# The first microseconds of a two-layer encoder kernel: matmuls of ones, two requests on ACT's queue, and squares and lambda moved

## The chip, the cores and the metric

The kernel runs on one core of a Trainium2 chip. The core has a matrix engine (PE, with its weight loads shown apart as PEld), a vector engine (DVE), a scalar engine (ACT), GpSimd (POOL) and a sequencer that mostly issues transfers (SP). Each runs its own instructions in order and waits for the others by semaphores. The metric is the device time of one execution in microseconds. The kernel before takes 1100.9 us, the median of three runs from 1099.71 to 1102.21.

## What is computed

The input is 512 tokens of 1024 features. Two layers follow each other, each a mixer and an MLP with squared ReLU, with an RMS norm ahead of each and a norm at the end. All of it is float32. Cut to what matters:

```
h = rmsnorm(x, norm_mix[0])                  # even layer
q, k, v, u = split(h @ ab_w_in)
p = softmax(q1 k1) - lam * softmax(q2 k2)    # 4 heads, block-causal
lam = exp(sum(l0*l1)) - exp(sum(l2*l3)) + lam_init
x = x + concat(subln(p @ v), pool_mixer(u)) @ ab_w_out
x = x + relu(rmsnorm(x) @ w1)**2 @ w2
h = rmsnorm(x, norm_mix[1])                  # odd layer: gated linear attention (GLA)
q, k, v, g, gk = split(h @ gla_w_in)
log_a = log_sigmoid(gk @ w_up + b) / 16      # decay per key feature
o = chunked_linear_attention(q, k, v, cumsum(log_a))
x = x + (rmsnorm(o) * silu(g)) @ gla_w_out
x = x + relu(rmsnorm(x) @ w1)**2 @ w2
return rmsnorm(x, norm_final)
```

The norm's factor for a token is the same for all features, so the kernel multiplies the raw `x` (times the gain) by the weights and puts the factor `rb` on the product when it leaves PSUM.

## The kernel before

**Tiling.** `x` is held transposed, as 8 tiles of 128 features x 512 tokens, numbered by `f`. A product of two float32 matrices is made of three matmuls of a reduced type: each operand is split into a high part and the rest, and `mm3` (L149 to L151) issues high x high, high x rest and rest x high into one PSUM bank. ACT makes the high parts (`wh` at L273 and L127, `row` at L181 and L187), DVE the rests (`wl` at L274 and L128, `row` at L182 and L188). A projection of one output tile (`proj_T`) is 8 x 3 = 24 matmuls of 512 columns; weights come from memory in blocks of 1 MB that hold two such tiles.

**The head.** The first weight block and `x` are requested by SP in pieces, alternately (L100 to L103): x0, w0, x1, w1, x2-3, w2-3, x4-5, w4-7, x6-7. The first part of `par` (gains and small constants) is requested on ACT's queue (L94), the second on SP's (L104). As the pieces land, ACT and DVE split them, and PE runs the first two output tiles of the q/k projection, feature tile by feature tile (`ps0`, 48 matmuls), then two more from the next block (`ps1`, L127/L128 and L149 to L151). Beside them ACT squares `x` (L244 and L238) and DVE adds the squares up (`nacc`, L247); `nrm.rb()` splits the sum (L203/L204), PE adds it over the partitions (L205/L206), ACT makes a reciprocal square root by Ln and Exp (L217, L218) and DVE refines it (L210 to L212). Then DVE evicts the four banks (L312), PE computes the scores (L326), and the v projection begins (L173 to L175), which needs free PSUM banks. Lambda's chain (L293 to L303) requests 128 KB on SP's queue behind two blocks of v weights.

**Order.** The code is a list in program order that a scheduler reorders by priorities and by a model of durations. `soon()` raises the priority, and `tc.issue_after(i)` keeps an instruction behind `i`. Scratch tiles of 128 x 512 come from buffer sets that are named `tmp` and `row`: the helper `tmp()` gives one from the one or the other set by turns, so each call to it decides for all later calls which set they fall into. When a buffer comes free is part of what the scheduler orders by.

**The GLA layer.** Its decays are made by Abs, Exp and Ln for four heads (L729 to L738), with table loads of ACT's functions between (L735, L740); scans (L745) add them up; `weights(h)` makes exponentials and products (L754, L765 to L773), and PE transposes one of the products (L776). At the layer's end the gate projection (24 matmuls for each of 8 tiles) is followed by its eviction (L898), Silu on ACT (L902) and the product with the normed output (L903), by a table load behind the last Silu (L905), by the split of 8 tiles for the output projection (L187/L188), and by that projection (`add_out(wo1, ...)`).

Of the kernel before, what the change touches and what calls it, by code (L numbers as in the profile page):

```python
# [9 lines left out]
F32 = mybir.dt.float32  # L10
F32R = mybir.dt.float32r
U8 = mybir.dt.uint8
AF = mybir.ActivationFunctionType
ALU = mybir.AluOpType
AX = mybir.AxisListType

P = 128
S = 512
D = 1024
KB = D // P  # L20
# [5 lines left out]
LAM_INIT = 0.2  # L26
# [4 lines left out]
C_SUB, C_PSC, C_BGK, C_GN, C_ICNT, C_ID = 40, 41, 45, 49, 57, 121  # L31
# [4 lines left out]
def trunk(ctx: ExitStack, tc: tile.TileContext, xT, par, lvl, lam4, wqk0, wu0, wv0, poolw, wo0,  # L36
          wgk, wup, wqk1, wv1, wg1, wo1, w1a, w2a, w1b, w2b, gfin, out):
    nc = tc.nc
    V, A, G, PE = nc.vector, nc.scalar, nc.gpsimd, nc.tensor
# [4 lines left out]
    def T(shape, tag, bufs, dt=F32):  # L44
        cnt[0] += 1
        return sb.tile(shape, dt, tag=tag, bufs=bufs, name=f"{tag}_{cnt[0]}")
# [6 lines left out]
    def turn(name, bufs):  # L53
        ring[name] = ring.get(name, -1) + 1
        return ring[name] % bufs

    def row(n=S, dt=F32):
        return T([P, n], "row", 54, dt)
# [17 lines left out]
    def tmp(n=S, dt=F32):  # L76
        if not mlp[0] and turn("tmp", 2):
            return row(n, dt)
        return T([P, n], "tmp", 4, dt)

    def PS(tag, shape=(P, S)):
        cnt[0] += 1
        return pp.tile(list(shape), F32, tag=tag, bufs=4, name=f"ps{tag}_{cnt[0]}")
# [9 lines left out]
    prm = T([P, N_PAR], "par", 1)  # L93
    nc.scalar.dma_start(prm[:, 0:C_ICNT], par[:, 0:C_ICNT])  # L94
    xall = T([P, KB, S], "x", 1)
    x = [xall[:, f, :] for f in range(KB)]
    turn("raw", 2)
    raw0 = raws[:, 0:4 * S].rearrange("p (a n) -> p a n", a=2)
    xT3 = xT.rearrange("(f p) s -> p f s", p=P)
    for f, nx, nw in ((0, 1, 1), (1, 1, 1), (2, 2, 2), (4, 2, 4), (6, 2, 0)):  # L100
        nc.sync.dma_start(xall[:, f:f + nx, :], xT3[:, f:f + nx, :])
        if nw:
            nc.sync.dma_start(raw0[:, :, f * P:(f + nw) * P], wqk0[0, :, :, f * P:(f + nw) * P])  # L103
    nc.sync.dma_start(prm[:, C_ICNT:], par[:, C_ICNT:])  # L104
    ident = prm[:, C_ID:C_ID + P]
    ones = T([P, P], "ones", 1)
    V.memset(ones, 1.0)
    ones_r = T([P, P], "onesr", 1, F32R)
    V.tensor_copy(ones_r, ones)
    A.preload_act_table_set("natural_log_exp_and_others")  # L110


    def load(src):
# [5 lines left out]
    ended = {}  # L119
# [24 lines left out]
    def act_tiles():  # L144
        return row(dt=F32R), row(dt=F32R)

    def mm3(ps, w, a, first, last):
        (wh, wl), (ah, al) = w, a
        PE.matmul(ps, wh, ah, start=first, stop=False)  # L149
        PE.matmul(ps, wh, al, start=False, stop=False)  # L150
        ended["mm"] = PE.matmul(ps, wl, ah, start=False, stop=last).ins  # L151

    def proj_T(w, act, tag="mm", ps=None, kbs=tuple(range(KB)), first=0, last=KB - 1):

        hi, lo = w
        ps = PS(tag) if ps is None else ps
        for kb in kbs:
            c = slice(kb * P, (kb + 1) * P)
            mm3(ps, (hi[:, c], lo[:, c]), act[kb], kb == first, kb == last)
        return ps  # L160
# [17 lines left out]
    def split_scaled(src, col, tiles=None):  # L178

        ah, al = tiles or act_tiles()  # L180
        A.activation(ah, src, AF.Copy, scale=col)  # L181
        V.scalar_tensor_tensor(out=al, in0=src, scalar=col, in1=ah.bitcast(F32), op0=ALU.mult, op1=ALU.subtract)  # L182
        return ah, al

    def split(src, tiles=None):
# [83 lines left out]
    for f in range(KB):  # L269
        if f < 2 or f % 2 == 0:  # L270
            c = slice(f * P, (f + (1 if f < 2 else 2)) * P)
            for j in range(2):
                A.activation(hl[j][0][:, c], raw0[:, j, c], AF.Copy)  # L273
                V.tensor_tensor(hl[j][1][:, c], raw0[:, j, c], hl[j][0][:, c].bitcast(F32), ALU.subtract)  # L274
        act.append(split_scaled(x[f], prm[:, C_MIX0 + f:C_MIX0 + f + 1]))
    ps0 = [PS("mm"), PS("mm")]
    for kb in range(KB):
        c = slice(kb * P, (kb + 1) * P)
        for j in range(2):
            mm3(ps0[j], (hl[j][0][:, c], hl[j][1][:, c]), act[kb], kb == 0, kb == KB - 1)  # L280
    st = Stream(wqk0, 2)
    ps1 = [proj_T(st.next(), act)]
    nrm = Norm()
    for f in range(KB):
        nrm.add(x[f])
    with tc.issue_after(ended["hi"]), tc.issue_after(ended["lo"]), tc.issue_after(ended["mm"]):
        rb = nrm.rb()
    first_sum = ended["sum"]
    ps1.append(proj_T(st.next(), act))


    l4 = tmp(256)
    nc.sync.dma_start(l4, lam4.partition_broadcast(P))  # L293
    lp = tmp(128).rearrange("p (a d) -> p a d", a=2)
    l4v = l4.rearrange("p (a b d) -> p a b d", a=2, b=2)
    V.tensor_tensor(lp, l4v[:, :, 0, :], l4v[:, :, 1, :], ALU.mult)
    consts = T([P, P], "lcol", 1)
    ls, le, neglam, sub8 = (consts[:, i:j] for i, j in ((0, 2), (8, 10), (16, 17), (24, 25)))
    V.tensor_reduce(out=ls, in_=lp, op=ALU.add, axis=AX.X)
    A.activation(le, ls, AF.Exp)  # L300
    V.tensor_tensor(neglam, le[:, 1:2], le[:, 0:1], ALU.subtract)
    V.tensor_scalar(out=neglam, in0=neglam, scalar1=-LAM_INIT, scalar2=None, op0=ALU.add)
    V.tensor_scalar(out=sub8, in0=prm[:, C_SUB:C_SUB + 1], scalar1=1.0 - LAM_INIT, scalar2=None, op0=ALU.mult)  # L303

    qk = {}

# [91 lines left out]
    def pooled(i, g):  # L398
        w = POOL_W[g]
        ps = proj_T(st.next(), act)  # L400
        u = row_u()
        G.memset(u[:, 0:16], 0.0)
        with soon():
            V.tensor_tensor(u[:, 16:], ps, rb, ALU.mult)
        s, step, us = u, 1, [row_u(), row_u()]
        while step < w:
            s2 = us[0]
            us.reverse()
            G.memset(s2[:, 0:16], 0.0)
            V.tensor_tensor(s2[:, 16:], s[:, 16:], s[:, 16 - step:16 + S - step], ALU.add)  # L410
            s, step = s2, 2 * step
        r = tmp2()
        V.scalar_tensor_tensor(out=r[:, 16:], in0=s[:, 32:], scalar=1.0 / w, in1=u[:, 32:], op0=ALU.mult,
                               op1=ALU.subtract)
        V.tensor_tensor(r[:, 0:16], s[:, 16:32], prm[:, C_ICNT + 16 * g:C_ICNT + 16 * (g + 1)], ALU.mult)
        V.tensor_tensor(r[:, 0:16], r[:, 0:16], u[:, 16:32], ALU.subtract)
        psy = PS("ax")
        PE.matmul(psy, pw[:, g, :], r, start=True, stop=True)
        cat[NH + i] = split_scaled(psy, prm[:, C_PSC + g:C_PSC + g + 1], (row16(dt=F32R), row16(dt=F32R)))
# [10 lines left out]
    def add_out(arr, src, col, late):  # L430


        st = Stream(arr)
        n, nxt = Norm(), []
        kbs = tuple(kb for kb in range(KB) if kb != late)
        ws = [st.next(), st.next()]
        pss = [proj_T(w, src, kbs=kbs, first=kbs[0], last=late) for w in ws]
        for w, ps in zip(ws, pss):
            proj_T(w, src, ps=ps, kbs=(late,), first=kbs[0], last=late)
        for f in range(KB):  # L440
            ps = pss[f] if f < 2 else proj_T(st.next(), src)
            with soon():
                V.tensor_tensor(x[f], x[f], ps, ALU.add)
                nxt.append(split_scaled(x[f], prm[:, col + f:col + f + 1]))
            n.add(x[f])
        return nxt, n
# [222 lines left out]
    act, nrm = add_out(wo0, cat, C_FFN0, NH - 1)  # L669
# [8 lines left out]
    act, nrm = ffn(w1a, w2a, act, nrm, C_MIX1)  # L678
# [12 lines left out]
    for kb in range(KB):  # L691
        for j in range(2):
            PE.matmul(psg, gk2[kb // 4][:, kb % 4, :, :].rearrange("p a b -> p (a b)"), act[kb][j],
                      start=kb == 0 and j == 0, stop=kb == KB - 1 and j == 1)
# [46 lines left out]
    for e, m in zip(es, ms):  # L741
        b = row16()
# [165 lines left out]
    act, nrm = add_out(wo1, oh, C_FFN1, KB - 1)  # L908
# [86 lines left out]
```

## Time and profile before

| | |
|---|---|
| runs | 1100.9 us median, 1099.71 to 1102.21 |
| profiled execution | 1100.49 us, of which the span (first to last instruction) is 1098.7 us |
| PE busy | 1071.5 us, 98% of the span |
| DVE, ACT busy | 825.5 us, 540.9 us |
| bytes moved | 103.53 MB, 94 GB/s over the span |
| PE idle, windows 0 to 35 us | 7.3 us, of which 4.85 ahead of its first matmul |

The span is nearly all matrix work, so time can only come out of the few places where PE stands still or runs at a lower clock, and go into new ones. Times of rows are microseconds from the span's start. A matmul of 512 columns is shown as 0.39 us long, but they follow each other every 0.227 us.

### The profile page before, as it was taken

What the parts mean: (1) busy time and instruction counts of PE and PEld (TensorE: products, weight loads), DVE (VectorE), ACT (ScalarE), POOL (GpSimd) and SP (SyncE); (2) the same over time, 40 slices, a digit from 0 to 9 for tenths busy, and PEclk for the clock granted to TensorE, in tenths of its full rate; (3) what the DMA queues carried; (4) which work ended last, traced back from release to release, by engine and by line L of the source; (5) the groups of instructions that cost most, each with busy time, mean ns of one, the idle gap of its engine ahead of it and who ended that gap; (6) DMA issues with size and microseconds to landing.
All of it is one profiled execution on the core that took longest, in us unless ns stands there. A gap on an engine that the chain in (4) does not pass through costs nothing.

```text
span 1098.7 us, 12896 instructions
## 1 busy us (share of the span) xinstructions
PE 1071.5 (98%) x4968; PEld 863.5 (79%) x4968; DVE 825.5 (75%) x1234; ACT 540.9 (49%) x894; POOL 2.3 (0%) x20
## 2 busy tenths in 40 slices
PE   7999889999999999999999999999999999999997
PEld 5676558888888888888887778788888888888885
DVE  6747747696498498498869887775696696696696
ACT  6444435455354354354655466854553453453454
POOL 0000000000000000000000000000000000000000
PEclk9999989999999999999999999999999999999999
DMA  7222223213314314302222121333205206206102
GB/s 239 82 84 108 82 77 124 88 39 136 132 39 153 116 39 154 115 17 84 108 77 77 39 86 39 146 115 115 96 1 209 98 1 224 83 1 229 39 1 78
DMA packets 17918, 103.53 MB, mean 94 GB/s; under 512 B 2016, under 2 KB 3040, under 8 KB 6208
## 3 DMA queue, kind: packets, MB, share of 16 engines
q1 hardware_dynamic: 17712, 102.67, 26.0%
q8 instruction: 39, 0.64, 0.2%
q14 instruction: 23, 0.19, 0.1%
q10 hardware_dynamic: 144, 0.03, 0.0%
HBM read 100.59 MB, written 2.10 MB: 93 GB/s over the span
## 4 chain that ended last, share of the span: by engine, by line
PE 90%; ACT 4%; DVE 4%; issue 1%; DMA 1%; SPq 0%; DVEq 0%; ACTq 0%
PE psmm L150 14%; PE psmm L149 14%; PE psmm L151 14%; PE psmm L571 6%; PE psmm L572 6%; PE psmm L573 6%; PE psax L151 3%; PE psax L149 3%; PE psax L150 3%; PE psax L573 2%; PE psax L571 2%; PE psax L572 2%; PE psmm L174 2%; PE psmm L173 2%; PE psmm L175 2%; PE psax L326 1%
## 5 line engine op out<-in xcount | busy, mean ns | idle before, releaser
L127 ACT ACTIVATE wh<-wraw 128x1024 fp32r<-128x1024 f32 x230 | 243.5, 1061 | 393.4 <-PE psmm L150 160.3
L128 DVE TENSOR_TENSOR wl<-wraw,wh 128x1024 fp32r<-128x1024 f32 x230 | 280.3, 1220 | 66.3 <-ACT wh L127 62.7
L149 PE MATMUL psmm<-row,wh 128*128 128x512 f32 x736 | 289.7, 394 | 15.0 <-ACT row L187 9.0
L150 PE MATMUL psmm<-row,wh 128*128 128x512 f32 x736 | 290.0, 394 | 0.1
L151 PE MATMUL psmm<-row,wl 128*128 128x512 f32 x736 | 288.5, 392 | 0.6 <-DVE wl L128 0.6
L149 PEld LDWEIGHTS psmm<-row,wh 128*128 128x128 f32 x736 | 138.7, 189 | 46.0 <-ACT row L187 10.1
L150 PEld LDWEIGHTS psmm<-row,wh 128*128 128x128 f32 x736 | 138.8, 189 | 31.8 <-issue 1.8
L151 PEld LDWEIGHTS psmm<-row,wl 128*128 128x128 f32 x736 | 138.9, 189 | 30.5 <-issue 1.1
L571 PE MATMUL psmm<-wh,row 128*128 128x512 f32 x320 | 124.6, 389 | 0.0
L573 PE MATMUL psmm<-wl,row 128*128 128x512 f32 x320 | 124.5, 389 | 0.0
L572 PE MATMUL psmm<-wh,row 128*128 128x512 f32 x320 | 124.5, 389 | 0.0
L546 DVE TENSOR_TENSOR wraw<-wraw 128x1024 f32<-128x1024 f32 x64 | 77.2, 1217 | 0.3
L498 DVE TENSOR_TENSOR row<-row,row 128x512 fp32r<-128x512 f32 x112 | 74.7, 682 | 0.3 <-ACT row L497 0.3
L572 PEld LDWEIGHTS psmm<-wh,row 128*128 128x128 f32 x320 | 60.1, 188 | 12.5
L573 PEld LDWEIGHTS psmm<-wl,row 128*128 128x128 f32 x320 | 60.1, 188 | 12.5
L571 PEld LDWEIGHTS psmm<-wh,row 128*128 128x128 f32 x320 | 60.1, 188 | 12.4
L497 ACT ACTIVATE row<-row 128x512 fp32r<-128x512 f32 x112 | 65.8, 618 | 5.3 <-DVE row L524 5.3
L512 DVE SCALAR_TENSOR_TENSOR tmp<-psmm,rb 128x512 f32<-128x512 f32 x48 | 32.9, 685 | 45.7 <-PE psmm L151 45.7
L517 ACT ACTIVATE row<-tmp 128x256 f32<-128x256 f32 x128 | 45.8, 405 | 10.9 <-DVE tmp L512 10.6
L151 PE MATMUL psax<-row,wl 128*128 128x512 f32 x128 | 49.8, 389 | 0.0
L149 PE MATMUL psax<-row,wh 128*128 128x512 f32 x128 | 49.8, 389 | 0.0
L150 PE MATMUL psax<-row,wh 128*128 128x512 f32 x128 | 49.8, 389 | 0.0
(235 smaller groups left out, 1312.6 us busy)
## 6 DMA issues: line engine op xcount, KB each, us to landing
wraw<-in_w1a SPq DMA_DIRECT2D x16, 1024.0 KB, 4.8
wraw<-in_w2a SPq DMA_DIRECT2D x16, 1024.0 KB, 4.8
wraw<-in_w1b SPq DMA_DIRECT2D x16, 1024.0 KB, 4.8
wraw<-in_w2b SPq DMA_DIRECT2D x16, 1024.0 KB, 4.8
wraw<-in_wo SPq DMA_DIRECT2D x8, 1024.0 KB, 4.8
wraw<-in_wqk SPq DMA_DIRECT2D x7, 1024.0 KB, 4.9
wraw<-in_wv SPq DMA_DIRECT2D x6, 1024.0 KB, 4.8
wraw<-in_wg SPq DMA_DIRECT2D x4, 1024.0 KB, 4.8
```

The source lines that it names most:

```text
L127: ended["hi"] = A.activation(hi, src, AF.Copy).ins
L128: ended["lo"] = V.tensor_tensor(lo, src, hi.bitcast(F32), ALU.subtract).ins
L149: PE.matmul(ps, wh, ah, start=first, stop=False)
L150: PE.matmul(ps, wh, al, start=False, stop=False)
L151: ended["mm"] = PE.matmul(ps, wl, ah, start=False, stop=last).ins
L497: A.activation(hi, src, AF.Copy)
L498: V.tensor_tensor(lo, src, hi.bitcast(F32), ALU.subtract)
L517: A.activation(raw[name][:, j, :], r[:, th * 256:th * 256 + 256], AF.Square)
L546: V.tensor_tensor(out[k], in0[k], in1[k], ALU.subtract)
L571: PE.matmul(ps[t], hi, wh[:, cs], start=f, stop=False, skip_group_check=True)
L572: PE.matmul(ps[t], lo, wh[:, cs], start=False, stop=False, skip_group_check=True)
L573: PE.matmul(ps[t], hi, wl[:, cs], start=False, stop=l, skip_group_check=True)
```

## The change

Four things are done in the head. The requests for x2 and x3 are made apart, and those for w0 and w1 move from SP's queue to ACT's, behind `par`. The request for lambda's vectors moves up behind x6-7, into a buffer taken directly from `tmp`'s set rather than by the helper `tmp()`. Thirty matmuls of ones (128 x 128 x 128) are issued ahead of everything on PE. The squares, and lambda's chain, which is now written ahead of `nrm.rb()`, are kept behind the last split of the first 8 tiles.

```
-    for f, nx, nw in ((0, 1, 1), (1, 1, 1), (2, 2, 2), (4, 2, 4), (6, 2, 0)):
+    for f, nx, nw in ((0, 1, 1), (1, 1, 1), (2, 1, 2), (3, 1, 0), (4, 2, 4), (6, 2, 0)):
         nc.sync.dma_start(xall[:, f:f + nx, :], xT3[:, f:f + nx, :])
         if nw:
-            nc.sync.dma_start(raw0[:, :, f * P:(f + nw) * P], wqk0[0, :, :, f * P:(f + nw) * P])
+            q = nc.scalar if f < 2 else nc.sync
+            q.dma_start(raw0[:, :, f * P:(f + nw) * P], wqk0[0, :, :, f * P:(f + nw) * P])
+    l4 = T([P, 256], "tmp", 4)
+    nc.sync.dma_start(l4, lam4.partition_broadcast(P))
     nc.sync.dma_start(prm[:, C_ICNT:], par[:, C_ICNT:])
...
+    WARM = 30
     A.preload_act_table_set("natural_log_exp_and_others")
+
+    psw = PS("ax", (P, P))
+    for i in range(WARM):
+        PE.matmul(psw, ones_r, ones_r, start=True, stop=True)
...
+        ended["ah"] = A.activation(ah, src, AF.Copy, scale=col).ins
+        ended["al"] = V.scalar_tensor_tensor(out=al, in0=src, scalar=col, in1=ah.bitcast(F32), op0=ALU.mult,
+                                             op1=ALU.subtract).ins
...
+    last_split = ended["ah"], ended["al"]
     ps1 = [proj_T(st.next(), act)]
     nrm = Norm()
-    for f in range(KB):
-        nrm.add(x[f])
+    with tc.issue_after(last_split[0]), tc.issue_after(last_split[1]):
+        for f in range(KB):
+            nrm.add(x[f])
+
+        lp = tmp(128).rearrange("p (a d) -> p a d", a=2)
...
     with tc.issue_after(ended["hi"]), tc.issue_after(ended["lo"]), tc.issue_after(ended["mm"]):
         rb = nrm.rb()
     first_sum = ended["sum"]
     ps1.append(proj_T(st.next(), act))
-
-
-    l4 = tmp(256)
-    nc.sync.dma_start(l4, lam4.partition_broadcast(P))
-    lp = tmp(128).rearrange("p (a d) -> p a d", a=2)
```

Lines of the changed kernel are 8 or 9 higher than those of before (L181 becomes L189, L187 becomes L196). The rows below are the instructions of one engine in the order in which it runs them, with the numbers of the tiles.

On ACT, at the program's start, there stood before:

```order
L94 DMA par_62<-in_par 128x57
L110 ACT_TABLE_LOAD
L181 ACTIVATE row_88<-x_64,par_62 128x512
L273 ACTIVATE wh_80<-wraw_61 128x128
L273 ACTIVATE wh_82<-wraw_61 128x128
L244 ACTIVATE nacc_216<-x_64 128x512
L181 ACTIVATE row_96<-x_64,par_62 128x512
```

and now:

```order
L94 DMA par_62<-in_par 128x57
L104 DMA wraw_61<-in_wqk 128x2x128 x2
L114 ACT_TABLE_LOAD
L282 ACTIVATE wh_114<-wraw_61 128x128
L282 ACTIVATE wh_116<-wraw_61 128x128
L189 ACTIVATE row_122<-x_64,par_62 128x512
L282 ACTIVATE wh_114<-wraw_61 128x128
```

Two requests stand ahead of the table load, the two weight casts ahead of the first split of `x`, and the first square is gone from between.

Further down in the head, ACT had the Ln (L217) of the first norm ahead of the third cast of the v weights, which is the first half of the second v block:

```order
L203 ACTIVATE row_241<-nacc_216 128x512
L127 ACTIVATE wh_503<-wraw_61 128x1024
L127 ACTIVATE wh_531<-wraw_61 128x1024
L217 ACTIVATE rb_239<-psax_240 128x512
L127 ACTIVATE wh_560<-wraw_61 128x1024
L218 ACTIVATE rb_239<-rb_239 128x512
```

and now:

```order
L212 ACTIVATE tmp_283<-nacc_250 128x512
L135 ACTIVATE wh_535<-wraw_61 128x1024
L135 ACTIVATE wh_563<-wraw_61 128x1024
L304 ACTIVATE lcol_275<-lcol_275 128x2
L135 ACTIVATE wh_592<-wraw_61 128x1024
L226 ACTIVATE rb_281<-psax_282 128x512
L227 ACTIVATE rb_281<-rb_281 128x512
```

That cast (`wh_592`) is now in front of the Ln (L226).

The one call less to `tmp()` turns the sets for every scratch tile behind it, and the order changes in the GLA layer, 1000 instructions away. On ACT, at the layer's end, there stood before:

```order
L187 ACTIVATE row_5686<-row_5286 128x512
L127 ACTIVATE wh_5822<-wraw_61 128x1024
L187 ACTIVATE row_5690<-row_5298 128x512
L902 ACTIVATE wraw_61<-wraw_61 128x512
L905 ACT_TABLE_LOAD
L187 ACTIVATE row_5694<-row_5336 128x512
L187 ACTIVATE row_5698<-row_5348 128x512
L187 ACTIVATE row_5702<-row_5386 128x512
L187 ACTIVATE row_5706<-row_5398 128x512
```

and now:

```order
L196 ACTIVATE row_5710<-row_5268 128x512
L135 ACTIVATE wh_5854<-wraw_61 128x1024
L910 ACTIVATE wraw_61<-wraw_61 128x512
L913 ACT_TABLE_LOAD
L196 ACTIVATE row_5714<-row_5280 128x512
L196 ACTIVATE row_5718<-row_5318 128x512
L196 ACTIVATE row_5722<-row_5330 128x512
L196 ACTIVATE row_5726<-row_5368 128x512
L196 ACTIVATE row_5730<-row_5380 128x512
L196 ACTIVATE row_5734<-row_5418 128x512
L196 ACTIVATE row_5738<-row_5430 128x512
```

Before, four of the eight splits for the output projection ran ahead of the last Silu; now one does, and seven stand behind the table load. PE meets them behind the last matmul of the gate projection (into `psmm_5667`):

```order
L159 MATMUL psmm_5667<-row_4068,wl_5664 128x512
L157 MATMUL psmm_5751<-row_5710,wh_5743 128x512
L157 MATMUL psmm_5773<-row_5710,wh_5747 128x512
L157 MATMUL psmm_5821<-row_5710,wh_5817 128x512
L157 MATMUL psmm_5858<-row_5710,wh_5854 128x512
L158 MATMUL psmm_5751<-row_5711,wh_5743 128x512
L159 MATMUL psmm_5751<-row_5710,wl_5744 128x512
L157 MATMUL psmm_5751<-row_5714,wh_5743 128x512
L158 MATMUL psmm_5773<-row_5711,wh_5747 128x512
L158 MATMUL psmm_5751<-row_5715,wh_5743 128x512
```

Six matmuls stand between that one and the first that reads `row_5714`; before, 19 stood between the gate projection's last and the first that reads a split from behind the table load (`row_5694`). At the layer's start, the transposes of the first head (L776, now L784) stand behind 59 instructions of PE counted from the first matmul of the values' projection (into `psmm_4549`), before behind 64; and ACT makes the decays of heads 1 and 3 with both table loads first, and those of heads 0 and 2 behind them, where before all four stood between the two loads.

More of the change, by code (lines that the diff above doesn't have):

```diff
@@ L180, in split_scaled @@
         ah, al = tiles or act_tiles()
-        A.activation(ah, src, AF.Copy, scale=col)
-        V.scalar_tensor_tensor(out=al, in0=src, scalar=col, in1=ah.bitcast(F32), op0=ALU.mult, op1=ALU.subtract)
+        ended["ah"] = A.activation(ah, src, AF.Copy, scale=col).ins
+        ended["al"] = V.scalar_tensor_tensor(out=al, in0=src, scalar=col, in1=ah.bitcast(F32), op0=ALU.mult,
+                                             op1=ALU.subtract).ins
         return ah, al
@@ L281, in trunk @@
     st = Stream(wqk0, 2)
+    last_split = ended["ah"], ended["al"]
     ps1 = [proj_T(st.next(), act)]
     nrm = Norm()
-    for f in range(KB):
-        nrm.add(x[f])
+    with tc.issue_after(last_split[0]), tc.issue_after(last_split[1]):
+        for f in range(KB):
+            nrm.add(x[f])
+        lp = tmp(128).rearrange("p (a d) -> p a d", a=2)
+        l4v = l4.rearrange("p (a b d) -> p a b d", a=2, b=2)
+        V.tensor_tensor(lp, l4v[:, :, 0, :], l4v[:, :, 1, :], ALU.mult)
+        consts = T([P, P], "lcol", 1)
+        ls, le, neglam, sub8 = (consts[:, i:j] for i, j in ((0, 2), (8, 10), (16, 17), (24, 25)))
+        V.tensor_reduce(out=ls, in_=lp, op=ALU.add, axis=AX.X)
+        A.activation(le, ls, AF.Exp)
+        V.tensor_tensor(neglam, le[:, 1:2], le[:, 0:1], ALU.subtract)
+        V.tensor_scalar(out=neglam, in0=neglam, scalar1=-LAM_INIT, scalar2=None, op0=ALU.add)
+        V.tensor_scalar(out=sub8, in0=prm[:, C_SUB:C_SUB + 1], scalar1=1.0 - LAM_INIT, scalar2=None, op0=ALU.mult)
     with tc.issue_after(ended["hi"]), tc.issue_after(ended["lo"]), tc.issue_after(ended["mm"]):
@@ L289, in trunk @@
     ps1.append(proj_T(st.next(), act))
-    l4 = tmp(256)
-    nc.sync.dma_start(l4, lam4.partition_broadcast(P))
-    lp = tmp(128).rearrange("p (a d) -> p a d", a=2)
[L295 to L303, printed above, removed]
     qk = {}
```

## The prediction

> **What bounds the kernel now.** I read the page first, then PE's timeline for its idle places, then the other engines' timelines at those places, and a table by stretches for the clock. The page says that PE is nearly always busy:
>
> ```profile
> PE 1071.5 (98%) x4968; PEld 863.5 (79%) x4968; DVE 825.5 (75%) x1234; ACT 540.9 (49%) x894; POOL 2.3 (0%) x20
> ```
>
> Of the span of 1098.7 us only some 27 are not PE's, so an edit pays only where PE stands or is slow, and costs wherever it makes PE stand anew. PE's timeline (start, length, and in brackets the idle time before and what ended it) shows the places in the head:
>
> ```profile
> 4.85 0.79 PE L149 MATMUL psmm<-row,wh 128*128 128x512 f32 x1 [4.85 <-ACT wh L273]
> ...
> 8.16 0.62 PE L150 MATMUL psmm<-row,wh 128*128 128x512 f32 x1
> 8.59 0.43 PE L151 MATMUL psmm<-row,wl 128*128 128x512 f32 x1
> 8.85 0.39 PE L149 MATMUL psmm<-row,wh 128*128 128x512 f32 x1
> 9.08 0.39 PE L150 MATMUL psmm<-row,wh 128*128 128x512 f32 x1
> ...
> 10.69 0.50 PE L149 MATMUL psmm<-row,wh 128*128 128x512 f32 x1 [0.98 <-ACT wh L273]
> ...
> 21.10 0.50 PE L151 MATMUL psmm<-row,wl 128*128 128x512 f32 x1 [0.57 <-DVE wl L128]
> ...
> 32.75 0.47 PE L173 MATMUL psmm<-wh,row 128*128 128x512 f32 x1 [0.93 <-ACT wh L127]
> 33.61 1.58 PE L326 MATMUL psax<-wraw 64*128 64x128 f32 x12
> ```
>
> The first nine matmuls follow each other every 0.43 us (8.16 to 8.59), later ones every 0.23 (8.85 to 9.08): PE starts at half its clock. The wait at 32.75 is put down to ACT; by the rows below the banks that it needs were evicted only then. ACT's timeline explains the others:
>
> ```profile
> 0.73 0.41 ACTq L94 DMA_DIRECT2D par<-in_par  x1
> 1.17 1.28 ACT L110 ACT_TABLE_LOAD   x1 [1.17 <-PEq L986]
> 3.87 0.72 ACT L181 ACTIVATE row<-x,par 128x512 fp32r<-128x512 f32 x1 [1.42 <-DMA par<-in_par]
> 4.50 0.49 ACT L273 ACTIVATE wh<-wraw 128x128 fp32r<-128x128 f32 x2
> ...
> 9.09 0.72 ACT L181 ACTIVATE row<-x,par 128x512 fp32r<-128x512 f32 x1 [1.76 <-DMA x<-in_xT]
> 9.71 0.61 ACT L238 ACTIVATE tmp<-x 128x512 f32<-128x512 f32 x1
> 10.23 0.71 ACT L273 ACTIVATE wh<-wraw 128x256 fp32r<-128x256 f32 x2
> ...
> 26.87 0.60 ACT L217 ACTIVATE rb<-psax 128x512 f32<-128x512 f32 x1 [0.80 <-PE psax L206]
> ...
> 28.31 0.62 ACT L218 ACTIVATE rb<-rb 128x512 f32<-128x512 f32 x1
> ```
>
> It waits 1.76 us for the common request of x2 and x3 (9.09), then squares x2 (9.71) before it casts the weights that PE waits for at 10.69.
>
> **The requests.** Rows of SP's timeline, and from the table of transfers the median time from issue to landing:
>
> ```profile
> 1.17 0.65 SPq L103 DMA_DIRECT2D wraw<-in_wqk  x1
> ...
> 3.09 0.60 SPq L101 DMA_DIRECT2D x<-in_xT  x1
> 3.73 0.55 SPq L103 DMA_DIRECT2D wraw<-in_wqk  x1
> ...
> wraw<-in_wqk SPq DMA_DIRECT2D x2, 128.0 KB, 3.3
> wraw<-in_wv SPq DMA_DIRECT2D x2, 1024.0 KB, 4.8
> ```
>
> A request occupies its issuer some 0.6 us. With w0 and w1 gone from SP, x2 is issued near 1.8 instead of 3.09, w2-3 near 2.4 instead of 3.73. On ACT the two requests (about 1.14 to 2.4) push the table load to end near 3.7, before w0 lands (1.15 + 3.3 = 4.5), so this delay is hidden; where w0 came earlier, it would cost up to 1.2. I let w0 land at 4.4: two casts of 0.3 each, then the split (3.87 to 4.50: 0.63), so PE's first real matmul comes near **5.5**, 0.65 later than now. The bytes ahead of w2-3 are the same but for x3, which now comes behind: w2-3 should land near 9.0, f2's matmuls begin near 9.4 to 9.6, **1.2 earlier** than 10.69. From there 36 matmuls of f2 to f7 run 8.2 us; the last ends near 17.7.
>
> [...]
>
> **The thirty matmuls.** No row shows them. The smallest with weights of their own that I found are transposes of the GLA layer:
>
> ```profile
> 580.36 0.55 PE L776 MATMUL psax<-par,tmp 128*128 128x128 f32 x3 [0.27 <-DVE tmp L773]
> ```
>
> The thirty can start when the ones are cast (near 1.3) and take at least 0.107 us each (a quarter of 0.43), 3.2 us in all. At most they take 0.37 (three transposes last 0.55 at full clock, and twice that at half) until the clock rises, by 8.6 as now, and then 0.18: they end near 10.4. The nearest row is that of a chain of matmuls with a weight load each that hides it (4.85 to 8.59), so I take 0.14 (4.2 us in all): they end near 5.5, no later than the inputs. At half clock 8 matmuls cost 8 x 0.2 = 1.6 us too much now, and these would go. Most of it is hidden, though: f0 and f1, warm, are done near 8.5 and PE then waits for w2-3 until 9.4. So warm-up is worth nothing beside the 1.2, within 0 and -0.7; at the far end of the bound the 48 matmuls of f0 to f7 (10.9 us) end near 21.3 instead of 17.7, and what the rests' coming at 19.9 doesn't hide of that, 1.4, is lost.
>
> **Squares and lambda.** Six squares of 0.52 us each (9.71 to 10.23) leave the stretch of ACT from 9 to 18. DVE's part of them comes to stand in front of the weights' rests:
>
> ```profile
> 19.22 0.69 DVE L247 SCALAR_TENSOR_TENSOR nacc<-tmp,nacc 128x512 f32<-128x512 f32 x1
> 19.83 2.35 DVE L128 TENSOR_TENSOR wl<-wraw,wh 128x1024 fp32r<-128x1024 f32 x2
> ...
> 29.59 0.68 DVE L210 SCALAR_TENSOR_TENSOR row<-psax,rb 128x512 f32<-128x512 f32 x1
> 30.20 0.28 DVE L296 TENSOR_TENSOR row<-tmp 128x128 f32<-128x128 f32 x1
> ...
> 31.91 2.48 DVE L312 TENSOR_TENSOR wraw<-psmm,rb 128x512 f32<-128x512 f32 x4
> ```
>
> Five additions of 0.69 (19.22) behind the last split, which DVE ends near 15.3, are done near 18.8 to 19.1, so the first rest is ready near 19.9 against 21.0 now. The matmul that waited for it (21.10) is followed by some 46 more at 0.227, to 31.6; with as many it is near 30.4 now. What follows waits for `rb`: the Ln is, in the changed order, queued behind the cast `wh_592`, which needs the second v block. That block is requested when the rests of `ps1` are made (near 21.3) and lands 4.8 later, 26.1; cast, Ln, Exp end near 28.3, DVE's three steps of 0.61 (29.59 to 31.91 are 2.3 us with lambda's 0.28 twice (30.20) between; these go) near 30.1: evictions begin **1.8 earlier**. In the changed order the scores stand ahead of the v projection's first matmuls: they follow two evictions of 0.62, near 31.3, and 1.5 us of scores (33.61) and three matmuls of 0.227 end near 33.5, where the same work ends near 35.1 now. **Head: -1.6 us**, between -0.8 (v block at 26.9, as late as now) and -2.4.
>
> **The GLA layer.** The flipped buffers change it. The rows at its end, of ACT, DVE and PE:
>
> ```profile
> 717.99 0.62 ACT L902 ACTIVATE wraw<-wraw 128x512 f32<-128x512 f32 x1
> 718.62 1.28 ACT L905 ACT_TABLE_LOAD   x1
> 719.91 2.19 ACT L187 ACTIVATE row<-row 128x512 fp32r<-128x512 f32 x4
> 717.16 0.68 DVE L898 TENSOR_TENSOR wraw<-psmm,rb 128x512 f32<-128x512 f32 x1
> 703.88 0.50 PE L205 MATMUL psax<-row,onesr 128*128 128x512 f32 x1 [0.76 <-ACT row L203]
> 721.33 0.50 PE L150 MATMUL psmm<-row,wh 128*128 128x512 f32 x1
> ```
>
> From the last gate eviction (717.16) to the first split behind the table load (719.91 + 0.5) are 3.3 us; PE's last gate matmul started 0.9 ahead of it (19 matmuls, then the one at 720.85, back by 0.227 each: 716.3). So the chain takes some 4.1, and PE has 19 matmuls, 4.3 us, to fill it. With six (1.4) it stands 2.5 us, and 0.3 more for the first rest from DVE, less the 0.25 that it waits now (721.33): 2.6. Four matmuls of 0.227 that the changed order has ahead of the last sums, not behind, may fill the idle 0.76 there (703.88). I take **+2.2**, between +1.8 and +2.9. At its start PE comes to the transposes of 580.36 about five matmuls (1.1 us) earlier and waited already. The chain gains some 0.5 on ACT, as table loads of 1.28 (718.62) move out of its way: **+0.6**, between 0 and +1.2. One table load more lies in ACT's own waiting time (it is busy for 49% of the span); where it has none, it costs its 1.28, which the upper ends hold.
>
> **The sum** on the profiled 1100.49 (0.4 under the median of the runs): -1.6 + 2.2 + 0.6 = +1.2, **1101.7**.
>
> **The clock.** A second unknown of about 1 us each way. By stretches (busy time of each engine, then PEclk, the granted share of full clock, here 0.62, 0.53 and 0.50; the last row is PE's timeline again):
>
> ```profile
> 134.00:138.00 4.00, 0.09 (x1) 0.09 (x1) 2.87 (x5) 0.93 (x2) 0.00 (x0) 0.62 0.00 0
> 138.00:142.00 4.00, 4.00 (x6) 1.88 (x7) 2.82 (x6) 0.36 (x1) 0.00 (x0) 0.53 0.00 0
> 152.00:155.40 3.40, 3.39 (x6) 1.47 (x7) 1.40 (x4) 0.00 (x0) 0.00 (x0) 0.50 0.00 0
> 137.91 0.79 PE L149 MATMUL psmm<-row,wh 128*128 128x512 f32 x1 [4.91 <-ACT row L187]
> ```
>
> After two long waits of the attention stage PE runs some 3.8 and 3.4 us at half clock, 3.6 us lost; if all comes 1.6 earlier, these places may cost a microsecond more or less. [...]
>
> **Rivals.** (a) *The GLA places cost nothing*: the changed order fills them, only the head counts: 1100.49 - 1.6 = 1098.9, with a lucky clock 1097.9. For it: the waits there now are 0.27 (580.36), 0.76 (703.88) and 0.25; against: the split that PE needs cannot come ahead of the last Silu. Chance 0.22. (b) *The second v block is late* and the Ln behind `wh_592` with it: from a landing at 27.9 on the head gains nothing, and each further microsecond is added whole; with the GLA's 2.8 that gives 1103.3, slower. For it: the block's request waits for rests that come to stand behind five additions; against: 4.8 us is steady. Chance 0.2. (c) *The warm-up misses*: real matmuls start cold at 5.5 and stay so up to 3.4 us, 7 x 0.2 = 1.4 us, of which the wait for w2-3 hides 0.9; or the thirty end only at 10.4 (+1.4): 1102.2 to 1103.1. [...] Chance 0.13. The forecast keeps 0.45.
>
> **The numbers.** A measurement of this kernel tells 0.2% (2.2 us) from no change. The forecast's own range, -2.4 + 1.8 - 1 to -0.8 + 4.1 + 1, is 1098.9 to 1104.8, most of it within 0.2%. Half of (a) and a little of the forecast is faster: 0.2; most of (b), a third of (c) and a quarter of the forecast slower: 0.3; the rest, 0.5, the same. The range, with part of (a): 1098.3 to 1104.5.
>
> **What would show it.** PE's first real matmul at 5.3 to 5.8 and at full pitch; f2 at 9.3 to 9.7; the first L312 (then L320) near 30.1 with the Ln behind `wh_592`; scores' end near 33.5; a wait of over 2 us behind the gate projection, ended by ACT's split. I would be wrong if no such wait shows, or if the attention stage's two waits change by over a microsecond.

## The result, and the profile after

The changed kernel takes 1108.3 us (median of 6 runs, 1106.52 to 1109.96), the kernel before 1101.71 us (6 runs, 1099.71 to 1102.55): 1.0063 of it, with a 95% interval of 1.0052 to 1.0073, or 6.6 us more. The forecast was 1101.7 us in a range up to 1104.5.

| | before | after |
|---|---|---|
| profiled execution | 1100.49 us | 1109.34 us |
| its span | 1098.7 us | 1107.5 us |
| PE busy | 1071.5 us | 1080.2 us |
| DVE busy, ACT busy | 825.5, 540.9 us | 825.8, 542.6 us |

PE is busy for 8.7 us longer. Of these, 6.7 are the thirty small matmuls (the first row below), which stand where PE only waited before. The other 2.0 are the same matrix work taking longer, so part of the loss isn't waiting but matmuls at a lower clock. PE's timeline of the changed kernel, in the head:

```profile
1.31 6.67 PE L118 MATMUL psax<-onesr 128*128 128x128 f32 x30 [1.31 <-DVE onesr L112]
7.77 0.73 PE L157 MATMUL psmm<-row,wh 128*128 128x512 f32 x1
...
9.41 0.63 PE L157 MATMUL psmm<-row,wh 128*128 128x512 f32 x1
9.84 0.63 PE L158 MATMUL psmm<-row,wh 128*128 128x512 f32 x1
...
11.12 0.42 PE L158 MATMUL psmm<-row,wh 128*128 128x512 f32 x1
11.38 0.40 PE L159 MATMUL psmm<-row,wl 128*128 128x512 f32 x1
11.61 0.40 PE L157 MATMUL psmm<-row,wh 128*128 128x512 f32 x1
...
33.07 1.58 PE L334 MATMUL psax<-wraw 64*128 64x128 f32 x12 [1.09 <-DVE wraw L320]
```

Each one of the thirty takes 0.215 us (1.31 to 7.77), and they do not raise the clock: the real ones behind them still follow each other every 0.43 us (9.41 to 9.84) up to 11.1. No wait is left between 7.77 and the scores at 33.07. These begin 0.5 us earlier than before (33.61), but only because the three matmuls of the v projection that stood ahead of them now follow: the fourth starts at 35.39, where it started at 35.12 before. So the head as a whole ends 0.3 us later in this execution, not earlier. Further on, the waits of the GLA layer, in PE's timeline again:

```profile
581.86 0.55 PE L784 MATMUL psax<-par,row 128*128 128x128 f32 x3 [1.07 <-DVE row L781]
...
696.51 0.50 PE L214 MATMUL psax<-tmp,onesr 128*128 128x512 f32 x1 [1.03 <-ACT tmp L212]
...
704.65 0.71 PE L873 MATMUL psax<-row,wraw 128*128 128x128 f32 x4 [1.49 <-DVE wraw L861]
...
709.11 0.44 PE L214 MATMUL psax<-tmp,onesr 128*128 128x512 f32 x1
...
722.03 0.47 PE L157 MATMUL psmm<-row,wh 128*128 128x512 f32 x1 [0.36 <-DVE wraw L906]
724.38 0.66 PE L158 MATMUL psmm<-row,wh 128*128 128x512 f32 x1 [1.88 <-DVE row L197]
```

These waits are 5.83 us together. Before, PE waits 0.27 us at the transposes, 0.71 and 0.76 us at the two column sums of the layer's end, and 0.08 us behind the gate projection. The second of these sums (L205, now L214 at 709.11) has no wait left; the 1.49 us at 704.65 is a new wait, ahead of matmuls of the outputs. The first of the sums before:

```profile
692.72 0.50 PE L205 MATMUL psax<-row,onesr 128*128 128x512 f32 x1 [0.71 <-ACT row L203]
```

Behind the last wait of the changed kernel, the table by stretches (length, then busy time and number of instructions of PE, PEld, DVE, ACT, POOL, then the granted clock, DMA share, GB/s):

```profile
722.00:724.50 2.50, 0.59 (x2) 0.31 (x3) 2.33 (x3) 2.47 (x4) 0.00 (x0) 1.00 0.15 29
724.50:728.00 3.50, 3.50 (x9) 2.72 (x10) 3.47 (x6) 3.12 (x6) 0.00 (x0) 0.51 0.93 372
728.00:732.00 4.00, 4.00 (x19) 3.28 (x18) 0.83 (x2) 0.00 (x0) 0.00 (x0) 1.00 0.43 180
```

PE is busy for 0.59 of 2.5 us, and then runs some 3.4 us at half clock: the row counts 9 matmuls, where 3.5 us at 0.227 each hold 15. This half-clock stretch is not in the profile of before, here over the same places:

```profile
724.00:730.00 6.00, 6.00 (x28) 4.99 (x27) 2.67 (x4) 2.90 (x4) 0.00 (x0) 1.00 0.26 111
```

The start of the same matmul in both profiles, counted back from PE's last, shows where the time goes without asking what a wait is. The changed kernel's execution is 0.4 us behind after the head, 2.0 after the attention stage, 4.3 at the last matmul of the gate projection (720.60 against 716.30), and 8.3 behind the half-clock stretch and from there to the end. So the GLA layer takes 6.3 us of it: 2.3 up to the end of the gate projection and 4.0 behind it.

### The profile page after: what moved, and what is told of

Read it like the earlier page. It is cut to its first block, busy times and chain, and to the rows that moved or that the text cites. A ratio compares the mean times of both kernels' runs of the same rounds, so it can differ in the third digit from the quotient of the medians.

```text
span 1107.5 us, 12961 instructions
## 1 busy us (share of the span) xinstructions
PE 1080.2 (98%) x4998; PEld 871.0 (79%) x4998; DVE 825.8 (75%) x1234; ACT 542.6 (49%) x895; POOL 2.3 (0%) x20
## 4 chain that ended last, share of the span: by engine, by line
PE 89%; DVE 6%; ACT 4%; DMA 1%; issue 1%; ACTq 0%; DVEq 0%
PE psmm L158 14%; PE psmm L159 14%; PE psmm L157 14%; PE psmm L580 6%; PE psmm L579 6%; PE psmm L581 6%; PE psax L159 3%; PE psax L157 3%; PE psax L158 3%; PE psax L579 2%; PE psax L580 2%; PE psax L581 2%; PE psmm L183 2%; PE psmm L181 2%; PE psmm L182 2%; PE psax L334 1%
```

## The experiments

### What costs: the flipped sets or the head

**e1_parity_back** is the changed kernel with one more turn of the scratch sets behind the head. From the first heads' softmax on, every engine then has the instructions of before in the same order.

```
     ps1.append(proj_T(st.next(), act))
+    turn("tmp", 2)
```

> The changed kernel with one more turn of the two scratch sets behind the head, so that everything behind the head has the order of before, and all four edits of the head stay. Theory A (the flipped sets cost the time, by the waits of the GLA layer and the half clock behind the longest one): the wait of about 2 us behind the gate projection is gone, PE's clock stays full there, and the time falls from 1108.3 to about 1102 (1101 to 1103). [...]

Measured: 1101.22 us against 1101.02 us for before, 1.0007 (0.9996 to 1.0018). **e2_flip_alone** is the reverse, the kernel before with that one line ahead of `qk = {}`:

> Before, with one more turn of the two scratch sets behind the head and nothing else. Theory A: the order of the GLA layer is that of the changed kernel, PE waits about 2 us behind the gate projection, then runs some 3.4 us at half clock, and the time rises by 5 to 7 us over before. Rival B: it rises by 2 us or less.

Measured: 1107.97 us, 1.0063 (1.0051 to 1.0075), the ratio of the whole change. PE's timeline and the stretch behind it show the changed kernel's end of the layer:

```profile
721.28 0.47 PE L149 MATMUL psmm<-row,wh 128*128 128x512 f32 x1 [0.41 <-DVE wraw L899]
723.58 0.79 PE L150 MATMUL psmm<-row,wh 128*128 128x512 f32 x1 [1.83 <-DVE row L188]
```

```profile
723.60:727.00 3.40, 3.40 (x8) 2.72 (x9) 3.23 (x6) 3.26 (x7) 0.00 (x0) 0.50 0.85 354
```

By the places of PE's matmuls this execution is 1.2 us behind ahead of the GLA layer, 3.5 at the end of the gate projection and 7.5 behind: 6.2 us in the layer, as in the changed kernel. So the edits of the head add nothing that can be measured, and the loss comes from one call less to `tmp()`. Theory A holds, and rival B, by which the head itself costs it, falls.

### What PE waits for at the end of the layer

**e5_load_last** takes the table load out of the chain that the prediction named (gate eviction, Silu, table load, split):

```
-    with tc.issue_after(last.ins):
-        A.preload_act_table_set("natural_log_exp_and_others")
-    oh = [split(ot[f], (row16(dt=F32R), row16(dt=F32R))) for f in range(KB)]
+    oh, lasts = [], []
+    for f in range(KB):
...
+    with ExitStack() as after_all:
+        for i in [last] + lasts:
+            after_all.enter_context(tc.issue_after(i.ins))
+        A.preload_act_table_set("natural_log_exp_and_others")
```

> The changed kernel with the table load behind the last Silu (L913) put behind the seven splits instead; nothing else moves on any engine. Theory A (PE's wait behind the gate projection is the chain gate eviction, Silu, table load, split, and the half clock behind it follows from that wait): the wait of 2.2 us shrinks by about 1.3 to 0.9 to 1.0, the 3.4 us at half clock behind it are gone, and the time falls from 1108 to about 1105 (3 us less). Rival G (the half clock has another cause, or the wait is for DVE's rests): the 3.4 us at half clock stay, and the time falls by 1.3 us or less.

Measured: 1108.63 us, 1.0063 (1.0051 to 1.0076): nothing gained. ACT's, DVE's and PE's timelines:

```profile
724.40 0.63 ACT L910 ACTIVATE wraw<-wraw 128x512 f32<-128x512 f32 x1
724.93 3.74 ACT L915 ACTIVATE row<-row 128x512 fp32r<-128x512 f32 x7
...
723.68 0.69 DVE L906 TENSOR_TENSOR wraw<-psmm,rb 128x512 f32<-128x512 f32 x1
724.35 1.23 DVE L136 TENSOR_TENSOR wl<-wraw,wh 128x1024 fp32r<-128x1024 f32 x1
725.49 0.68 DVE L911 TENSOR_TENSOR row<-row,wraw 128x512 f32<-128x512 f32 x1
726.09 4.90 DVE L916 TENSOR_TENSOR row<-row,row 128x512 fp32r<-128x512 f32 x8
...
726.83 0.68 PE L158 MATMUL psmm<-row,wh 128*128 128x512 f32 x1 [1.85 <-DVE row L916]
```

ACT's splits start right behind the Silu, and PE stands as long as ever, for DVE: gate eviction, the rest of a weight block, the last product with the gate, and only then the eight rests, the first of which PE needs. The same is to be seen in the changed kernel itself, where the wait of 1.88 us was ended by DVE's row (L197), not by ACT's. There DVE's and ACT's timelines are:

```profile
723.64 0.69 DVE L197 TENSOR_TENSOR row<-row,row 128x512 fp32r<-128x512 f32 x1
```

```profile
723.86 3.75 ACT L196 ACTIVATE row<-row 128x512 fp32r<-128x512 f32 x7
```

The rest at 723.64 is that of the one tile that ACT had split ahead of the last Silu (`row_5711` from `row_5710`). The fifth matmul behind the gate projection reads it, and the table load has no part in it. DVE's rest is done at 724.33 and the first of ACT's seven splits at 724.49. The two chains end within 0.2 us of each other, so taking the one away shows the other. Theory A's chain falls as the sole cause; rival G's second half holds.

**e9_splits_in_loop** moves both, ahead of the last Silu:

```
+    oh = []
     with tc.issue_after(last_exp[0]):
         for f in range(KB):
             last = A.activation(gts[f], gts[f], AF.Silu)
             V.tensor_tensor(ot[f], ot[f], gts[f], ALU.mult)
+            oh.append(split(ot[f], (row16(dt=F32R), row16(dt=F32R))))
...
-    oh = [split(ot[f], (row16(dt=F32R), row16(dt=F32R))) for f in range(KB)]
```

> The changed kernel with each split for the output projection written right behind its product with the gate, so that five splits and four of DVE's rests run ahead of the last Silu and the last gate eviction; the flipped sets stay. e5 showed that the table load isn't what PE waits for. Theory M (PE waits for DVE, whose eight rests all stand behind the last gate product, and the half clock follows from that wait): no wait over 0.5 us behind the gate projection, full clock there, and the time falls by 3.5 to 4.5 us under the changed kernel, to 1103.5 to 1105. Rival N (the half clock has another cause): the wait goes but 3.4 us at half clock stay, and the time falls by 2.2 us or less.

Measured: 1104.63 us, 1.0034 (1.0021 to 1.0048), 3.7 us under the changed kernel's median. PE's timeline, then the stretch behind:

```profile
722.89 0.50 PE L158 MATMUL psmm<-row,wh 128*128 128x512 f32 x1 [0.97 <-DVE row L197]
```

```profile
723.00:726.50 3.50, 3.50 (x15) 2.52 (x16) 2.33 (x4) 1.75 (x4) 0.00 (x0) 1.00 0.91 316
```

A wait of 0.97 us is left (under 0.5 was expected), the clock stays full (1.00), and 15 matmuls run in 3.5 us where 9 did. Theory M holds but for the size of the wait that is left: the half clock goes with the wait, and its own part of the loss is about 1.7 us, half of the 3.4. By the places of PE's matmuls 1.1 us are lost behind the gate projection, where the changed kernel lost 4.0; the wait accounts for 1.3 of the difference and the clock for the rest.

**e6_parity_back_later** turns the sets back between the decays and the first head's weights:

```
+    turn("tmp", 2)
     weights(0)
```

> The changed kernel with one more turn of the two scratch sets just ahead of the first head's weights in the GLA layer, behind the decays; three splits then run ahead of the last Silu, not one. Theory A (what costs is that only one split runs ahead of the last Silu): no wait over 0.6 us behind the gate projection, full clock there, and the time is 1101.5 to 1103.5. Rival H (the flipped decays at the layer's start cost the most, by waits that are passed on): the time stays above 1105.

Measured: 1103.52 us, 1.0017 (1.0009 to 1.0026), the upper edge of what theory A had. The wait at the layer's start is still 1.08 us, that behind the gate projection is gone (718 to 726 us without a wait, at a granted clock of 1.00). Rival H falls: the flipped decays cost 1.6 us at most (1103.52 less the 1101.96 of before), the flip of `weights` and what is allocated behind it the other 5.

### The head: requests and ones

With the sets turned back, the head's edits can be taken off one by one. **e3_parity_back_sp** (`q = nc.sync` for all pieces):

> e1 with the requests for w0 and w1 back on SP's queue. Theory C (on ACT's queue w0 lands 5.2 us after its issue, 2 us later than from SP's, and nothing is won because the thirty matmuls hold PE to 7.7 anyway): w0 lands near 4.3, ACT's first cast starts near 4.4 instead of 6.42, but PE's first real matmul still starts at 7.6 to 7.8 and the time is that of e1 within 1 us. Rival D (w0's landing sets PE's start): the first real matmul starts at 5 to 6 and the time is 1 to 2 us under e1.

**e4_parity_back_sp_no_ones** (e3 with `WARM = 0`):

> e3 without the thirty matmuls of ones. Theory E (they occupy PE to 7.7 without raising its clock): PE's first real matmul starts near 5, its clock rises when it does in before, near 8.3 to 11.7, and the eighth feature tile's matmuls end 1 to 2 us earlier than in e3; the time is 0 to 1 us under e3, since the eviction of the first banks is set by the second v block. Rival F (they do raise the clock in most executions): the time is 1 us or more above e3.

**e10_parity_back_no_ones** (e1 with `WARM = 0`):

> e1 without the thirty matmuls of ones, with w0 and w1 still on ACT's queue. Theory C (w0's landing near 6.3 holds PE there as long as the ones do): PE's first real matmul starts at 7.3 to 7.8, as in e1, its clock rises at 10 to 11.5, and the time is that of e1 within 1 us. Rival D (the ones hold PE): it starts at 5 to 6.

| | queue of w0, w1 | ones | ACT's first cast | first real matmul | last two splits of x | time | ratio to before |
|---|---|---|---|---|---|---|---|
| e1 | ACT | 30 | 6.33 | 7.77 | 12.77 | 1101.22 | 1.0007 (0.9996 to 1.0018) |
| e3 | SP | 30 | 4.54 | 7.77 | 13.53 | 1102.52 | 1.0015 (1.0006 to 1.0023) |
| e4 | SP | none | 4.41 | 4.75 | 15.10 | 1101.77 | 1.0004 (0.9996 to 1.0013) |
| e10 | ACT | none | 4.84 | 6.02 | 12.63 | 1101.32 | 1.0003 (0.9994 to 1.0011) |

The places are those of the profiled executions, in us. w0 comes by ACT's queue in time for a cast at 4.8 to 6.3 here, by SP's at 4.4 to 4.5; the last pieces come earlier when ACT's queue is used. With the same requests w0 took 3.5 to 5.2 us to land by ACT's queue in six profiles, so the first cast moves from one execution to the next. The first real matmul moves by 3 us between these kernels, and the time by 1.3 us at most, with intervals that overlap: what follows (the first rest of the next weights, the sums, the second v block) takes it up. What takes it up was not tested piece by piece. e3 starts as theory C said (4.54 and 7.77), and rival D falls; but its time is 1.3 us above that of e1, not within 1. Theory C's "7.3 to 7.8" for e10 was a miss, since w0 landed earlier in that execution than in e1; its rival's "5 to 6" was met but for 0.02, so without the ones PE is held by the inputs alone. e4's first matmul and its time are those of theory E and rival F falls, but it does not finish f0 to f7 earlier (the last of these 48 matmuls starts at 19.99, in e3 at 20.08); its inputs came later.

The profiled executions of e1 and e3 differ by 2.4 us, and a part of it is the clock behind the attention stage, whose two long waits are the same in both. The tables by stretches of e1, then of e3:

```profile
138.50:141.00 2.50, 2.50 (x5) 1.33 (x5) 2.17 (x5) 0.00 (x0) 0.00 (x0) 0.50 0.00 0
141.00:144.00 3.00, 3.00 (x12) 1.93 (x11) 0.75 (x1) 1.16 (x2) 0.00 (x0) 0.98 0.00 0
```

```profile
138.50:141.00 2.50, 2.50 (x4) 1.21 (x5) 2.33 (x6) 0.00 (x0) 0.00 (x0) 0.50 0.00 0
141.00:144.00 3.00, 3.00 (x5) 1.35 (x4) 1.25 (x2) 0.69 (x1) 0.00 (x0) 0.50 0.00 0
```

The wait ended at 137.77 in e1 and at 138.43 in e3; the clock came back near 141.1 in the one and not before 144.0 in the other. That is half clock for 3.3 and for at least 5.6 us, so e3's execution lost 1.1 us more here. It came there 0.7 us later, but that is no rule: e10's wait ended at 137.10, earlier than e1's, and its half clock lasted to 142.6, for 5.5 us. The two waits and the clock behind them cost between 0.4 us less and 1.8 us more than in the profile of before, over all thirteen other profiles; none of the edits was made there.

**e11_before_requests** is the kernel before with only the requests changed, the other way round (w0, w1 by SP, w2-3 and w4-7 by ACT):

```
-    for f, nx, nw in ((0, 1, 1), (1, 1, 1), (2, 2, 2), (4, 2, 4), (6, 2, 0)):
+    for f, nx, nw in ((0, 1, 1), (1, 1, 1), (2, 1, 2), (3, 1, 0), (4, 2, 4), (6, 2, 0)):
...
+            q = nc.sync if f < 2 else nc.scalar
```

> Before, with x2 and x3 requested one by one and w2-3 and w4-7 requested on ACT's queue, w0 and w1 kept on SP's. Theory P (the second queue brings the later pieces sooner and the first piece later: in the changed kernel the last split started 2.8 us earlier, but the first 3 us later): w0 lands near 4.3 and PE's first matmul stays at 4.9, the last split of x starts 1 to 2 us earlier than in before (15.57), f0 to f7 end 1 us earlier; the time is 0 to 1 us under before. Rival Q (the requests are bound by the bytes): the last split stays within 0.5 us of 15.57.

Measured: 1102.05 us, 1.0007 (0.9998 to 1.0016). ACT's and SP's timelines:

```profile
1.17 1.27 ACTq L104 DMA_DIRECT2D wraw<-in_wqk  x2
...
7.32 0.51 ACT L274 ACTIVATE wh<-wraw 128x128 fp32r<-128x128 f32 x2 [3.56 <-DMA wraw<-in_wqk]
...
1.17 0.64 SPq L104 DMA_DIRECT2D wraw<-in_wqk  x1
```

w0, issued at the same 1.17 as before and by the same queue, is cast at 7.32, not at 4.50, because two larger requests went out beside it; that x2 and x3 are requested one by one is not the reason, since in e3 and e4, with all pieces on SP's queue, it is cast at 4.41 to 4.54. PE's first real matmul starts at 8.49 instead of 4.85, and the last split of x at 16.52 instead of 15.57. Theory P falls: with w2-3 and w4-7 asked for sooner on the second queue, the piece that is needed first came 2.8 us later. Rival Q's "within 0.5 us" is missed too. The time hardly follows: 3.6 us at the first matmul are 0.9 us behind the head in this execution.

### The ones: thirty of them don't raise the clock

**e8_before_wide_ones** puts 8 matmuls of 512 columns of ones ahead of PE's first real one in the kernel before: by theory J such wide ones raise the clock, by rival K ones don't, whatever their width. The diff is also that of the next kernel but for the count and the place:

```
+    wide = T([P, S], "tmp", 4)
+    V.memset(wide, 1.0)
+    wide_r = T([P, S], "row", 54, F32R)
+    V.tensor_copy(wide_r, wide)
+    psw = PS("ax")
+    for i in range(8):
+        PE.matmul(psw, ones_r, wide_r, start=True, stop=True)
```

> Before, with 8 matmuls of ones of 512 columns ahead of PE's first real one and nothing else. Theory J: they run from about 1.5 to 5, the clock rises at 5 to 8.5 instead of 8.3 to 11.7, and the time is 0 to 1 us under before, because f2 waits for its inputs (10.7) and the first eviction for the sums. Rival K: the clock rises as late as in before and the time is the same or up to 0.5 us more.

Measured: 1101.11 us against 1101.96 us, 0.9997 (0.9989 to 1.0006). PE's timeline:

```profile
2.05 3.78 PE L117 MATMUL psax<-row,onesr 128*128 128x512 f32 x8 [2.05 <-DVE row L114]
5.63 0.63 PE L155 MATMUL psmm<-row,wh 128*128 128x512 f32 x1
6.05 0.63 PE L156 MATMUL psmm<-row,wh 128*128 128x512 f32 x1
6.48 0.58 PE L157 MATMUL psmm<-row,wl 128*128 128x512 f32 x1
6.90 0.39 PE L155 MATMUL psmm<-row,wh 128*128 128x512 f32 x1
7.13 0.40 PE L156 MATMUL psmm<-row,wh 128*128 128x512 f32 x1
...
11.11 0.50 PE L155 MATMUL psmm<-row,wh 128*128 128x512 f32 x1 [1.99 <-ACT wh L279]
```

The clock is full from 6.9 on (the next matmul starts 0.23 us later, at 7.13), 1.3 us behind the first real matmul (before: 3.8 us behind it). The times that theory J gives for its rise, 8.3 to 11.7 for before among them, were the author's estimate. What that wins is given back at once: the wait for f2's weights is 1.99 us where it was 0.98.

**e7_wide_ones** is e3 with 16 such matmuls in place of the thirty:

> e3 with 16 matmuls of ones of 512 columns in place of 30 of 128 columns, of the same length together (16 x 0.43 = 6.8 us). [...]

Measured: 1110.16 us, 1.0077 (1.0064 to 1.0090). As a time it says nothing on theory J, since the scheduler put the cast of the wide ones behind weight rests on DVE: the ones ran from 13.63 to 19.64 and held up everything. But its first real matmuls, behind nothing but ones, follow each other every 0.23 us (they start at 19.64, 19.87 and so on). So ones count, if they have 512 columns: rival K falls. In none of the six profiles with thirty narrow ones was the clock full at the first real matmul (7.77), though those ones had run for 6.5 us.

**e12_before_requests_wide_ones** joins e11 and e8:

> e11 with the 8 matmuls of ones of 512 columns of e8. If the earlier inputs let PE use the higher clock, f0 to f7 end 1 us earlier than in e11 and the time is 0.5 to 1.5 us under before; if the first eviction still waits for the sums and the second v block, the time is that of e11 within 0.5 us.

Measured: 1102.28 us, 1.0005 (0.9996 to 1.0014), that of e11 within 0.5 us. The ones run from 2.05 us, and then PE waits 3.45 us for its inputs, to 9.28. Its first ten real matmuls follow each other every 0.43 us, so nothing was left of what the ones could have won, where in e8 the clock stayed full through a wait of 1.99 us (11.11). This is not a test of whether a full clock helps with these requests. None of the twelve is faster than the kernel before.

## Why the prediction was wrong

**The GLA layer's end: the wait was right, its consequence was missed.** The prediction sized the wait behind the gate projection at 2.6 us and took 2.2; it was 0.36 + 1.88, less the 0.08 of before, 2.16. Its chain was half the truth, and that the size came out is in part luck. It let PE run six matmuls and then wait for ACT's split behind the table load. PE ran three, waited 0.36 us ahead of the fourth for DVE's last gate eviction, and then ahead of the fifth for DVE's first rest; DVE's chain only happens to be as long as ACT's table load and split (e5). The step that failed is the price: it treated a wait as its own length, and kept the clock as "about 1 us each way" at the attention stage. Here the wait itself brings 3.4 us at half clock, 1.7 us more (e9 takes away the half clock with 1.3 us of the wait). No run shows a term of 1 us each way that follows from coming earlier: over the thirteen other profiles the attention stage's two waits and the clock behind them cost between 0.4 us less and 1.8 us more than before.

In the changed kernel 2.24 us of waiting, with PE busy for 0.59 of 2.5 us, were enough for the clock to fall (0.51 behind them). The prediction's own row fits: 0.62 over 134 to 138 us is half clock for the last 3.0 of 4.0 us, which puts the fall some 2 us into the wait of 4.91 us. But 2 us are not enough everywhere: in the next wait there, of 4.05 us, the granted clock reads 1.00 from 148 to 152 us and 0.50 only from 152 on. The half clock lasted some 3.4 us behind the gate projection and 3.4 us in the prediction's row 152 to 155.4, but at least 5.6 us in e3's attention stage. In e5's execution a wait of 2.89 us ahead of the scores had the same consequence: the twelve matmuls behind it take 2.94 us, in the changed kernel 1.58:

```profile
34.32 2.94 PE L334 MATMUL psax<-wraw 64*128 64x128 f32 x12 [2.89 <-DVE wraw L320]
```

**The sums and outputs ahead of it: one place was right, the next was overlooked.** "Four matmuls ... may fill the idle 0.76 there": they did, no wait is left at the last sums. But the wait at the sums before them grew from 0.71 to 1.03 us, and a new one of 1.49 us stands at 704.65, where matmuls of the outputs wait for DVE (L861). In all 1.05 us more, where the prediction had put nothing or a gain.

**The layer's start** was right: +0.6 predicted, 1.07 - 0.27 = 0.8 measured. Its gain on ACT shows too: against the 2.0 us by which all is late there, the exponential that the transposes wait for (577.93 before, 579.50 now) came 0.4 us sooner; 0.5 was predicted.

Together these are 2.16 + 1.7 + 1.05 + 0.8 = 5.7 us where the prediction had 2.8. By the places of PE's matmuls the layer takes 6.3 us in the changed kernel and 6.2 in e2, so the layer is the whole of the 6.6 but for 0.3. The 0.6 between the 5.7 and the 6.3 is in waits and slower stretches of the layer that are not told apart here. The attention stage's clock moves single executions by more than that, as said above, the changed kernel's profiled one by 1.6 us.

**The head: -1.6 predicted, nothing measured** (e1: 1.0007). This is the second step that failed. In the six profiles with w0 and w1 on ACT's queue PE is between 0.8 us ahead of the profile of before (e10) and 2.6 us behind it (e5) after the head, never 1.6 ahead. Three of its terms were off. w0 was let land at 4.4 by ACT's queue; its cast came at 6.42. By the table of transfers w0 and w1 took a median of 5.4 us to land by ACT's queue in the changed kernel, 3.3 by SP's in the kernel before:

```profile
wraw<-in_wqk ACTq DMA_DIRECT2D x2, 128.0 KB, 5.4
```

ACT's queue brought the last pieces sooner: their splits begin 0.76 us earlier in e1 than in e3, about one request of 0.65. The first piece came later: its cast was 1.8 us behind in e1 against e3 and 0.3 in e10. The ones were sized at 0.14 us each and took 0.215, to 7.77, without raising the clock: rival (c), at no cost that e10 shows (1.0003 of before without them, 1.0007 with them), since PE's waits for inputs and weights of before (0.98, 0.57) went in exchange. And the second v block was let land at 26.1. It was requested at 21.53, near the 21.3 of the prediction, but took 5.7 us to land in the changed kernel and 7.2 in e5's execution, where the prediction called 4.8 steady. ACT's timeline of the changed kernel, then of e5's profiled execution:

```profile
27.30 1.06 ACT L135 ACTIVATE wh<-wraw 128x1024 fp32r<-128x1024 f32 x1 [1.74 <-DMA wraw<-in_wv]
28.27 0.58 ACT L226 ACTIVATE rb<-psax 128x512 f32<-128x512 f32 x1
```

```profile
28.55 1.06 ACT L135 ACTIVATE wh<-wraw 128x1024 fp32r<-128x1024 f32 x1 [3.23 <-DMA wraw<-in_wv]
29.52 0.58 ACT L226 ACTIVATE rb<-psax 128x512 f32<-128x512 f32 x1
```

The Ln waits behind that cast, as the prediction had it, but the cast starts at 26.2 to 28.6 in the five profiles with the whole head of the changed kernel, so evictions begin at 30.6 to 33.0 (31.73 in the changed kernel, 31.91 before), not at 30.1. Rival (b) named this; in e5's execution it made PE wait the 2.89 us ahead of the scores. In the median it is a wash (e1), not the cause of the loss. Rival (a), that the GLA order costs nothing, was the furthest off.

## What to carry to other kernels

Where scratch buffers alternate, adding or dropping one allocation can reorder work a thousand instructions later; turn the alternation back and time that kernel beside the change, before the change itself is judged. A wait of PE can cost more than its length: in these profiles a wait of 1.99 us left the clock full, while 2.24 us in two pieces were followed by some 3.4 us at half clock, which cost 1.7 us more, and 2.89 us by scores that took 2.94 us where they take 1.58. Here such a wait ended earlier only when the chains of both engines to that place were shortened (e5, with ACT's alone: 1.85 us left; e9, with both: 0.97). In this head, which waits for its inputs, a full clock (e8, 0.9997 of before) or an earlier or later first piece (e10, 1.0003; e11, 1.0007) moved the wait and hardly the end.

## What the runs showed of the hardware that was not expected

- Thirty matmuls of 128 columns, back to back for 6.5 us, did not raise PE's clock in any of six profiles; 8 of 512 columns, followed by 1.3 us of real ones, did within 4.9 us (e8), and 16 did alone (e7); 8 with a wait of 3.45 us behind them left the next ten real ones at half clock (e12). What it is in the width that decides was not shown.
- The clock fell behind waits of 2.24 us (the changed kernel, granted 0.51 from 724.5 to 728 us; e2, 0.50; e2 and e5 have the wait within 0.01 us) and 2.89 us (e5, by the 2.94 us of the scores), and stayed full behind 1.49 us (704.65; 1.00 over 690 to 720 us) and 1.99 us (e8; 0.23 us from one matmul to the next from 11.45 on).
- Two requests on a second queue delayed a request issued at the same time on the first: w0's cast at 7.32 (e11), not 4.50.
- The granted clock reads 1.00 in the first stretch of the changed kernel, where matmuls of 512 columns follow each other every 0.43 us:

```profile
7.70:11.20 3.50, 3.50 (x10) 2.53 (x10) 3.50 (x8) 3.50 (x9) 0.00 (x0) 1.00 1.03 384
11.20:14.00 2.80, 2.80 (x14) 2.29 (x13) 2.80 (x8) 2.80 (x8) 0.00 (x0) 1.00 1.02 375
```

Eight matmuls start in the 3.5 us there, twelve in the 2.8 us behind (the rows also count those that reach in from ahead). At this program's start the clock is therefore read from the matmuls' pitch, not from this column.
